# Running products of the forget gates: two scan instructions for a pair of heads in place of twelve products by doubling

## The chip, the cores and the metric

The kernel runs on one core of a Trainium2 chip. The metric is the device time of one launch in microseconds; before the change the median of three timed runs is 845.55 us (845.29 to 845.63). In the profile the engines are PE (matrix products; PEld is its weight load), DVE (vector), ACT (activation), POOL (general purpose) and SP, which here only issues transfers.

## The reference

Two layers over 512 tokens of width 1024, inner width 2048. Layer 0 is a pooling mixer. Layer 1, in which the change lies, is a gated linear recurrence (HGRN2) with 16 heads of 128 channels:

```python
def hgrn2_mixer(h, w_in, lb, norm_g, w_out):
    u = h @ w_in
    q, fz, i, gate = jnp.split(u, 4, axis=-1)
    log_f = jnp.logaddexp(jnp.log(lbf), jnp.log1p(-lbf) + jax.nn.log_sigmoid(fz))  # f = lb + (1 - lb) * sigmoid(fz)
    k = (1.0 - lbf) * jax.nn.sigmoid(-fz)
    ...
    # o_t = S_t^T q_t,  S_t = diag(f_t) S_{t-1} + k_t v_t^T, for each head, v = i
    o = hgrn2_chunk_scan(qc, kc, vc, bc)
    o = o * rsqrt(mean(o * o, over the head) + EPS) * norm_g
    return (o * jax.nn.silu(gate)) @ w_out
```

Around each mixer there are an RMSNorm before it and a residual addition after it, and a last RMSNorm.

## The kernel before

Activations lie with channels on the 128 partitions and the 512 tokens along the free axis. Each large product of float32 numbers is done as three products of exact halves (`mm3`, L126 to L128). Weights come in pieces of 128x1024 that SP loads (`wraw`), that ACT casts to the high half (`whi`, L94), and from which DVE subtracts it for the low half (`wlo`, L95). A piece's load and split carry a priority 300 traced instructions ahead of their use (`AHEAD`).

The program is written in an order, and a planner (the Tile layer) then lays down each engine's queue from the order, the dependences and the priorities; every engine works its own queue in order.

Layer 1 goes over four groups of four heads. `prepare(g)` makes what the heads of group g need: `forget` projects the gates' inputs, applies two sigmoids (ACT, L338 and L340) and lets `store` write the gates `f` (DVE, L505, L506, L508; POOL L507); then come the running products of `f`; then `queries` projects q. `group(g)` projects the values (`inputs`), runs the heads (`within` L549 to L558, `state`, `attend`), and, behind the first two heads' `gated`, calls `prepare(g + 1)`. `prepare(0)` stands alone ahead of the first group. Output products of the group before (`project_out`, the `z1` halves) fill PE meanwhile.

Tokens are taken in four blocks of 128, each with two halves of 64. Within a block the decay is a ratio to the block's middle, so the first half needs the products of the gates from t + 1 to the middle (backwards), the second those from the middle to t (forwards). Before the change these are made in place by doubling, for a pair of heads at a time: for h = 1, 2, 4, 8, 16, 32 one product for the first halves (L519) and one for the second (L520), each on 256 elements a partition, twelve in all. What follows reads them: POOL copies the products over whole halves to `ends` (L524, L525) and multiplies by the block's first gate (`e`, L527); POOL clips them at `FLOOR` (L533), DVE takes the reciprocal `r` (L534); `f` and `r` then scale k (POOL, L536 and L537) and q (DVE, L538 and L539), which the heads' first products on PE (L549) take.

Of the kernel before, what the change touches and what calls it, by code (L numbers as in the profile page):

```python
"""Two-layer streaming-encoder trunk: multi-scale causal pooling mixer, then HGRN2, on one core.

Activations are kept channel-major ([channel, token]), so every projection contracts over
partitions.  float32 products with long moving operands run as three one-pass float32r products of
exact halves (x = hi + lo, 12 significant bits each): hi*hi + hi*lo + lo*hi.  Short ones run as
plain float32 products.

The RMSNorm factor of a token commutes with the projection, so it is applied where the projection's
result leaves PSUM.

HGRN2 is computed as causal linear attention.  The decay between tokens s < t is the product of the
forget gates of s+1..t.

Factored form: within a block of 128 tokens the decay is a ratio of products taken to the block's middle,
one factor going to k and one to q; from block to block the state is carried.  The products over half a
block must not run out of range for this; whether they did is recorded on the way.

General form, for any gates, run over the layer when the record says so: a pair is served at the one
level h (1, 2, 4, ..) at which s and t lie in sibling blocks of h tokens; the decay is then (s to the end
of its block) * (start of t's block to t), both at most one, so nothing can overflow.  The running products  # L20
are lengthened from level to level by the sibling's total.
"""
# [10 lines left out]
F32 = mybir.dt.float32  # L33
# [4 lines left out]
ALU = mybir.AluOpType  # L38
PSUM = bass.MemoryType.PSUM

P = 128
# [3 lines left out]
KD = D // P          # 8 channel tiles of the model width  # L45
KI = DI // P         # 16 channel tiles of the inner width
NG = 4               # groups of the inner width
GC = DI // NG        # 512 channels a group
GT = GC // P         # 4 channel tiles a group
TB = T // P          # 4 token blocks  # L50
# [4 lines left out]
NORM_AT, SPREAD_AT = (KD - 2, 2), (KD - 1, 1)   # where in its first projection (step, tile)  # L55
AHEAD = 300           # how far, in traced instructions, the weights run ahead of their use
FLOOR = 1e-26         # the least product of gates over half a block that the factored form takes
LEVELS = (1, 2, 4, 8, 16, 32, 64)

# columns of the packed parameters  # L60
# [5 lines left out]
def trunk(ctx: ExitStack, tc: tile.TileContext, xT, par, ident_d, causal_d, mask_d, w0_in, w0_grp, w0_out, w1_in, w1_out, outT):  # L66
# [9 lines left out]
    # ---- parameters and constants  # L76
    ones = const.tile([P, P], F32, name="ones")
    nc.gpsimd.memset(ones, 1.0)
    # the tensor engine's clock comes up, and the function table in, while the first loads are on their way
# [17 lines left out]
    def piece(src):  # L97
        """A [128, 2, 512] piece of a weight as exact halves."""
        raw = wpool.tile([P, 2, GC], F32, name="wraw", tag="wraw", bufs=RAW)
        hi = wpool.tile([P, 2, GC], F32R, name="whi", tag="whi", bufs=WB)  # L100
        lo = wpool.tile([P, 2, GC], F32R, name="wlo", tag="wlo", bufs=WB)
        with tc.high_priority(AHEAD):
            nc.sync.dma_start(out=raw, in_=src)
            split(raw, hi, lo)
        return hi, lo

    def load_in(w, col=0):
        """512 columns of a projection: one pair of halves a row tile."""
        v = w.rearrange("(k p) n -> p k n", p=P)
        out = []  # L110
        for i in range(v.shape[1] // 2):
            hi, lo = piece(v[:, 2 * i:2 * i + 2, col:col + GC])
            out += [(hi[:, 0], lo[:, 0]), (hi[:, 1], lo[:, 1])]
        return out

    def load_out(w, g):
        """Rows of group g of a [2048, 1024] projection, one row tile a piece."""
# [12 lines left out]
    def project4(pieces, xs, norm):  # L130
        """The four channel tiles of 512 columns, advancing together through the contraction.  The norm's
        short products go in before the end, so that its result is there in time."""
# [11 lines left out]
    def project(pieces, n, xs):  # L144
        """[128 channels, 512 tokens] of a projection: columns n*128.. of the pieces."""
# [6 lines left out]
    def rms(name, srcs, cols=slice(0, T)):  # L152
        """1/rms of each token over the channel tiles, [token, block]."""
# [29 lines left out]
    def spread(rn):  # L183
        """[token, block] -> [any channel, token], in PSUM."""
# [31 lines left out]
    # ---- layer 0: pooling mixer  # L216
# [83 lines left out]
    # kept for the general form of the next layer  # L300
# [4 lines left out]
    # ---- layer 1: HGRN2 mixer  # L305
    # lower bounds of this layer: softmax over the layers, cumulated, less the first
# [14 lines left out]
    def hgrn(ctx, general):  # L321
# [4 lines left out]
        # attention weights within a token block: zeroed once, later only the causal part is written  # L326
# [16 lines left out]
        def forget(g, store):  # L343
            wf = None if g == 0 else load_in(w1_in, DI + g * GC)
            fs, ks = [], []
            for pr in range(2):
                f = l1.tile([P, 2, T], F32, name="f", tag="f", bufs=2)
# [46 lines left out]
        def normed(o, so):  # L394
            """Each token of a head divided by its rms; so is left with the sums of squares."""
# [13 lines left out]
        def gated(g, n, on, gate, last):  # L409
            """Back to [channel, token], times the norm's weight and the gate."""  # L410
# [14 lines left out]
        def group(g, prepare, heads, zs):  # L425
            """One group of heads: the rest of its projections, its heads, and the output products of the
            group before, which keep the tensor engine busy meanwhile."""
# [19 lines left out]
        def finish(zs):  # L447
            """Last output product and final norm, one half of the tokens after the other."""
# [11 lines left out]
            def scaled(half, i, bc, rb):  # L460
                """Two channel tiles of the result; the first two by way of the engines that are free."""
# [27 lines left out]
        def factored():  # L489
            """Decays within a block of 128 tokens as ratios to its middle; between blocks by the state.  # L490
            Returns how many of the marks that say that the ratios stayed in range are set."""
# [8 lines left out]

            def store(f, pr, j, hd, s1):
                """In a block's first half at t the gate of t + 1 (one in the middle), in the second that of t."""
                s, fv = halved(s1), halved(f[:, j])
                a = dict(scalar1=rest[:, hd:hd + 1], scalar2=low[:, hd:hd + 1], op0=ALU.mult, op1=ALU.add)
                nc.vector.tensor_scalar(out=fv[:, :, 0, 0:63], in0=s[:, :, 0, 1:64], **a)  # L505
                nc.vector.tensor_scalar(out=fv[:, :, 1, :], in0=s[:, :, 1, :], **a)  # L506
                nc.gpsimd.memset(fv[:, :, 0, 63:64], 1.0)  # L507
                nc.vector.tensor_scalar(out=cur["first"][pr][:, j], in0=s[:, :, 0, 0], **a)  # L508

            def prepare(g):  # L510
                cur["first"] = firsts = [l1.tile([P, 2, TB], F32, name="first", tag="first", bufs=2) for _ in range(2)]
                es = []
                fs, ks = forget(g, store)
                for pr in range(2):
                    f, kk = fs[pr], ks[pr]
                    for hh in (1, 2, 4, 8, 16, 32):
                        x = f.rearrange("p j (b s m two h) -> p (j b) s m two h", b=TB, s=2, two=2, h=hh)
                        n = 32 // hh
                        nc.vector.tensor_tensor(out=x[:, :, 0, :, 0], in0=x[:, :, 0, :, 0], in1=x[:, :, 0, :, 1, 0:1].broadcast_to([P, 2 * TB, n, hh]), op=ALU.mult)  # L519
                        nc.vector.tensor_tensor(out=x[:, :, 1, :, 1], in0=x[:, :, 1, :, 1], in1=x[:, :, 1, :, 0, hh - 1:hh].broadcast_to([P, 2 * TB, n, hh]), op=ALU.mult)  # L520
                    # products over the halves, the first with the block's first gate as well
                    en = ends[:, g * GT + 2 * pr:g * GT + 2 * pr + 2]
                    fv = f.rearrange("p j (b s c) -> p j b s c", b=TB, s=2)
                    nc.gpsimd.tensor_copy(out=en[:, :, :, 0], in_=fv[:, :, :, 0, 0])  # L524
                    nc.gpsimd.tensor_copy(out=en[:, :, :, 1], in_=fv[:, :, :, 1, 63])  # L525
# [4 lines left out]
                for pr in range(2):  # L530
                    for j in range(2):
                        r = l1.tile([P, T], F32, name="r", tag="r", bufs=2)
                        nc.gpsimd.tensor_scalar(out=r, in0=fs[pr][:, j], scalar1=FLOOR, scalar2=None, op0=ALU.max)  # L533
                        nc.vector.reciprocal(out=r, in_=r)  # L534
                        rv, fv, kv, qv = halved(r), halved(fs[pr][:, j]), halved(ks[pr][:, j]), halved(qs[pr][:, j])
                        nc.gpsimd.tensor_tensor(out=kv[:, :, 0], in0=kv[:, :, 0], in1=fv[:, :, 0], op=ALU.mult)  # L536
                        nc.gpsimd.tensor_tensor(out=kv[:, :, 1], in0=kv[:, :, 1], in1=rv[:, :, 1], op=ALU.mult)  # L537
                        nc.vector.tensor_tensor(out=qv[:, :, 0], in0=qv[:, :, 0], in1=rv[:, :, 0], op=ALU.mult)  # L538
                        nc.vector.tensor_tensor(out=qv[:, :, 1], in0=qv[:, :, 1], in1=fv[:, :, 1], op=ALU.mult)  # L539
                cur["k"], cur["q"], cur["e"] = ks, qs, es  # L540

            def within(n):
                """Weights within the blocks; the tokens after the middle do not weigh on those before."""
# [229 lines left out]
```

## Time and profile before

| | |
|---|---|
| median of three timed runs | 845.55 us (845.29 to 845.63) |
| the profiled execution: span from its first to its last instruction | 844.7 us |
| so between the profiled span and the median | 0.85 us |
| instructions in the profile | 10684 |
| busy share of the span | PE 98%, PEld 82%, DVE 65%, ACT 33%, POOL 20% |
| HBM traffic | 92 GB/s over the span |

The span is what the views below divide up; the timed runs contain a little more than it. Busy shares are means over the whole span. Matrix products overlap, so PE is busy also where one product follows the other at the slower of two paces.

### The profile page before, as it was taken

The numbers are of one execution on the slowest core, as the hardware profiler recorded it, in microseconds if no ns is written. First come the engines' busy times: TensorE is split into PE (matmuls) and PEld (weight loads), VectorE is DVE, ScalarE is ACT, GpSimd is POOL, SyncE is SP. The second block draws the span as 40 slices with busy tenths as digits, with TensorE's granted clock in tenths as the row PEclk, the third lists the DMA queues.
The fourth block names the chain that finished last, engine by engine and source line by source line (L and its number), as shares of the span: only waits on it lengthen the run. The fifth ranks groups of instructions, "written<-read, shape, count | busy, mean of one in ns | idle before, by whom it ended". The sixth has DMA issues, their size and how long they took to land.

```text
span 844.7 us, 10684 instructions
## 1 busy us (share of the span) xinstructions
PE 829.0 (98%) x4134; PEld 691.7 (82%) x4134; DVE 550.5 (65%) x845; ACT 274.6 (33%) x472; POOL 171.7 (20%) x218
## 2 busy tenths in 40 slices
PE   9899999999999999999999999999999999999995
PEld 7688888888888888888888888888888888888895
DVE  7766645754685465799269963279963279963643
ACT  7352224213333144323332232332332332334231
POOL 5020001001002023170314300315300305203024
PEclk9999999999999999999999999999999999999997
DMA  6622333123423145133033331233331133320203
GB/s 217 209 70 84 99 100 100 55 96 100 150 99 100 54 163 180 57 95 105 1 100 100 100 100 30 71 100 100 99 101 39 62 100 100 100 100 1 74 2 104
DMA packets 37931, 78.56 MB, mean 93 GB/s; under 512 B 2800, under 2 KB 5104, under 8 KB 37872
## 3 DMA queue, kind: packets, MB, share of 16 engines
q1 hardware_dynamic: 35744, 74.98, 27.9%
q10 hardware_dynamic: 2128, 2.81, 0.9%
q8 instruction: 34, 0.56, 0.3%
q14 instruction: 25, 0.20, 0.1%
HBM read 73.59 MB, written 4.19 MB: 92 GB/s over the span
## 4 chain that ended last, share of the span: by engine, by line
PE 91%; DVE 4%; DMA 2%; POOL 1%; issue 1%; ACT 1%; SPq 0%; ACTq 0%; DVEq 0%; POOLq 0%
PE mm L126 28%; PE mm L128 27%; PE mm L127 27%; PE a L587 2%; DVE wlo L95 1%; PE a L549 1%; PE a L589 1%; PE a L567 1%; DVE r L534 1%; DMA wraw<-in_w0i 1%; PE a L414 1%; PE a L556 1%; DMA h<-in_xT 0%; DMA wraw<-in_w1i 0%; PE a L188 0%
## 5 line engine op out<-in xcount | busy, mean ns | idle before, releaser
L126 PE MATMUL mm<-xh,whi 128*128 128x512 f32 x640 | 251.3, 393 | 0.9 <-DVE v L242 0.4
L128 PE MATMUL mm<-xh,wlo 128*128 128x512 f32 x640 | 249.8, 391 | 1.6 <-DVE wlo L95 1.6
L127 PE MATMUL mm<-xl,whi 128*128 128x512 f32 x640 | 249.6, 390 | 0.0
L94 ACT CAST whi<-wraw 128x1024 fp32r<-128x1024 f32 (+1 forms) x140 | 141.8, 1025 | 249.8 <-PE mm L127 168.9
L95 DVE TENSOR_TENSOR wlo<-wraw,whi 128x1024 fp32r<-128x1024 f32 (+1 forms) x140 | 173.4, 1265 | 58.2 <-ACT whi L94 57.2
L128 PEld LDWEIGHTS mm<-xh,wlo 128*128 128x128 f32 x640 | 120.4, 188 | 28.6 <-DVE wlo L95 3.2
L126 PEld LDWEIGHTS mm<-xh,whi 128*128 128x128 f32 x640 | 120.6, 188 | 26.6 <-ACT whi L94 1.1
L127 PEld LDWEIGHTS mm<-xl,whi 128*128 128x128 f32 x640 | 120.5, 188 | 24.5
L214 DVE TENSOR_TENSOR h<-mm,h 128x512 f32<-128x512 f32 x56 | 38.5, 689 | 62.8 <-PE mm L128 62.5
L534 DVE RECIPROCAL r<-r 128x512 f32<-128x512 f32 x16 | 53.5, 3341 | 1.5 <-POOL r L533 1.5
L126 PE MATMUL mm<-zh,whi 128*128 128x512 f32 x128 | 50.4, 394 | 0.0
L128 PE MATMUL mm<-zh,wlo 128*128 128x512 f32 x128 | 50.2, 392 | 0.0
L126 PE MATMUL mm<-whi,xh 128*128 128x512 f32 x128 | 50.1, 391 | 0.0
L127 PE MATMUL mm<-wlo,xh 128*128 128x512 f32 x128 | 49.8, 389 | 0.0
L128 PE MATMUL mm<-whi,xl 128*128 128x512 f32 x128 | 49.8, 389 | 0.0
L127 PE MATMUL mm<-zl,whi 128*128 128x512 f32 x128 | 49.7, 388 | 0.0
L390 POOL TENSOR_TENSOR gs<-fz,s 128x512 f32<-128x512 f32 x16 | 20.7, 1293 | 98.6 <-ACT s L388 98.6
L272 POOL TENSOR_TENSOR gs<-gt,sg 128x512 f32<-128x512 f32 x16 | 21.2, 1328 | 91.7 <-ACT sg L270 91.5
L126 PE MATMUL mm<-z1h,whi 128*128 128x512 f32 x96 | 38.2, 398 | 0.0
L128 PE MATMUL mm<-z1h,wlo 128*128 128x512 f32 x96 | 38.0, 395 | 0.0
L127 PE MATMUL mm<-z1l,whi 128*128 128x512 f32 x96 | 38.0, 395 | 0.0
L402 POOL TENSOR_TENSOR ro<-mo,mhalf 128x4 f32<-128x4 f32 x16 | 16.2, 1015 | 104.0 <-DVE mo L400 104.0
(141 smaller groups left out, 1202.1 us busy)
## 6 DMA issues: line engine op xcount, KB each, us to landing
wraw<-in_w1i SPq DMA_DIRECT2D x64, 512.0 KB, 4.1
wraw<-in_w0i SPq DMA_DIRECT2D x28, 512.0 KB, 4.5
wraw<-in_w0o SPq DMA_DIRECT2D x16, 512.0 KB, 4.3
wraw<-in_w1o SPq DMA_DIRECT2D x16, 512.0 KB, 4.0
wraw<-in_w0g SPq DMA_DIRECT2D x8, 512.0 KB, 3.9
h<-in_xT SPq DMA_DIRECT2D x8, 256.0 KB, 5.1
wraw<-in_w0i SPq DMA_DIRECT2D x8, 256.0 KB, 5.0
hmid<-h ACTq DMA_DIRECT2D x8, 256.0 KB, 2.3
```

The source lines that it names most:

```text
L94: nc.scalar.copy(out=hi, in_=src)
L95: nc.vector.tensor_tensor(out=lo, in0=src, in1=hi, op=ALU.subtract)
L126: nc.tensor.matmul(out, lh, rh, start=start, stop=False)
L127: nc.tensor.matmul(out, lh, rl, start=False, stop=False)
L128: nc.tensor.matmul(out, ll, rh, start=False, stop=stop)
L214: nc.vector.tensor_tensor(out=h[n], in0=acc, in1=h[n], op=ALU.add)
L272: nc.gpsimd.tensor_tensor(out=gs, in0=gt, in1=sg, op=ALU.mult)
L390: nc.gpsimd.tensor_tensor(out=gs, in0=gt, in1=sg, op=ALU.mult)
L402: nc.gpsimd.tensor_tensor(out=ro[:, :, 0], in0=mo, in1=mhalf[:, :TB], op=ALU.pow)
L414: nc.tensor.transpose(out=oT[:, b * P:(b + 1) * P], in_=on[:, b], identity=ident)
L534: nc.vector.reciprocal(out=r, in_=r)
L587: nc.tensor.matmul(o[:, b], Ads[pr][:, j, t], v[:, b, n * P:(n + 1) * P], start=True, stop=b == 0)
```

## The change

The twelve products give way to two `tensor_tensor_scan` instructions on DVE, each over 512 elements a partition: one runs through the first halves of both heads from the last token back, one through the second halves forwards. A scan keeps a running value: at each element it multiplies the value by `data0` and adds `data1`. At the places where a new half begins, `data0` is 0 and `data1` holds the value to start from: a constant tile `middle` (1 at each half's last token) for the backward one, and for the forward one a tile `begins` in which `store` writes each second half's first gate. The zeros are written by POOL, two memsets for a pair of heads in place of one for each head (L507). `f` is now stored half by half, all first halves and then all second halves, so that each scan's 512 elements lie together; the readers of `f`, `r` and the ends follow that layout, with as many elements as before. `store` has one instruction more on DVE (the gates for `begins`, four elements), and L506 writes 252 elements and not 256.

Three tiles of 512 floats are new in layer 1's pool (`middle`, two `begins`), each cleared once by POOL. The scratch area for dynamic DMA is set to 1024 where the program is made, so all tiles lie at other addresses than before. Comments and docstrings are gone.

```diff
-        def forget(g, store):
+        def forget(g, store, shape=[P, 2, T]):
...
-                f = l1.tile([P, 2, T], F32, name="f", tag="f", bufs=2)
+                f = l1.tile(shape, F32, name="f", tag="f", bufs=2)
...
+            middle = l1.tile([P, 2 * TB * 64], F32, name="middle")
+            nc.gpsimd.memset(middle, 0.0)
+            nc.gpsimd.memset(middle.rearrange("p (b c) -> p b c", c=64)[:, :, 63:64], 1.0)
+            begins = [l1.tile([P, 2, TB, 64], F32, name=f"begin{i}") for i in range(2)]
+            for b in begins:
+                nc.gpsimd.memset(b, 0.0)
...
-                s, fv = halved(s1), halved(f[:, j])
+                s, fv, bv = halved(s1), f[:, :, j], cur["begin"][pr][:, j]
                 a = dict(scalar1=rest[:, hd:hd + 1], scalar2=low[:, hd:hd + 1], op0=ALU.mult, op1=ALU.add)
-                nc.vector.tensor_scalar(out=fv[:, :, 0, 0:63], in0=s[:, :, 0, 1:64], **a)
-                nc.vector.tensor_scalar(out=fv[:, :, 1, :], in0=s[:, :, 1, :], **a)
-                nc.gpsimd.memset(fv[:, :, 0, 63:64], 1.0)
+                nc.vector.tensor_scalar(out=fv[:, 0, :, 0:63], in0=s[:, :, 0, 1:64], **a)
+                nc.vector.tensor_scalar(out=fv[:, 1, :, 1:64], in0=s[:, :, 1, 1:64], **a)
+                nc.vector.tensor_scalar(out=bv[:, :, 0], in0=s[:, :, 1, 0], **a)
                 nc.vector.tensor_scalar(out=cur["first"][pr][:, j], in0=s[:, :, 0, 0], **a)
...
-                    for hh in (1, 2, 4, 8, 16, 32):
-                        x = f.rearrange("p j (b s m two h) -> p (j b) s m two h", b=TB, s=2, two=2, h=hh)
-                        n = 32 // hh
-                        nc.vector.tensor_tensor(out=x[:, :, 0, :, 0], in0=x[:, :, 0, :, 0], in1=x[:, :, 0, :, 1, 0:1].broadcast_to([P, 2 * TB, n, hh]), op=ALU.mult)
-                        nc.vector.tensor_tensor(out=x[:, :, 1, :, 1], in0=x[:, :, 1, :, 1], in1=x[:, :, 1, :, 0, hh - 1:hh].broadcast_to([P, 2 * TB, n, hh]), op=ALU.mult)
+                    back, on = (f[:, s].rearrange("p j b c -> p (j b c)") for s in range(2))
+                    nc.gpsimd.memset(f[:, 0, :, :, 63:64], 0.0)
+                    nc.gpsimd.memset(f[:, 1, :, :, 0:1], 0.0)
+                    nc.vector.tensor_tensor_scan(out=back[:, ::-1], data0=back[:, ::-1], data1=middle[:, ::-1], initial=0.0, op0=ALU.mult, op1=ALU.add)
+                    nc.vector.tensor_tensor_scan(out=on, data0=on, data1=begins[pr].rearrange("p j b c -> p (j b c)"), initial=0.0, op0=ALU.mult, op1=ALU.add)
...
-    nc = bacc.Bacc("TRN2", target_bir_lowering=False, num_devices=1)
+    nc = bacc.Bacc("TRN2", target_bir_lowering=False, num_devices=1, dynamic_dma_scratch_size=1024)
```

## Rows read from the trace of the kernel before

**Rows 1.** The page's first part: busy time, share of the span, instructions.

```profile
PE 829.0 (98%) x4134; PEld 691.7 (82%) x4134; DVE 550.5 (65%) x845; ACT 274.6 (33%) x472; POOL 171.7 (20%) x218
```

**Rows 2.** Busy time in stretches: length, then each engine's us, granted clock, DMA.

```profile
0.00:40.00 40.00, 34.41 (x145) 27.25 (x146) 28.61 (x38) 22.04 (x34) 12.95 (x18) 0.96 0.65 212
40.00:390.00 350.00, 350.00 (x1557) 288.46 (x1555) 228.48 (x313) 113.08 (x141) 56.45 (x86) 1.00 0.31 99
390.00:400.00 10.00, 9.73 (x95) 8.18 (x94) 8.44 (x24) 2.77 (x5) 0.00 (x0) 1.00 0.62 205
400.00:830.00 430.00, 430.00 (x2314) 363.55 (x2313) 281.39 (x463) 135.04 (x288) 98.75 (x109) 1.00 0.23 74
830.00:844.70 14.70, 4.89 (x31) 4.31 (x29) 3.61 (x10) 1.62 (x4) 3.58 (x5) 0.65 0.37 125
345.00:390.00 45.00, 45.00 (x211) 37.07 (x210) 43.38 (x67) 15.62 (x20) 18.70 (x20) 1.00 0.21 60
```

**Rows 3.** Waits of PE: us in total, times, longest.

```profile
PE a L549 <- ACT kt L558: 0.3, 1, 0.3
```

**Rows 4.** The chain of waits, 336 to 412 us: start, us, what.

```profile
366.11 1.61 issue
...
393.50 0.39 ACT kt L558
```

**Rows 5.** DVE's groups by line and shape: busy us, mean ns of one.

```profile
L534 DVE RECIPROCAL r<-r 128x512 f32<-128x512 f32 x16 | 53.5, 3341 | 1.5 <-POOL r L533 1.5
...
L519 DVE TENSOR_TENSOR f<-f 128x256 f32<-128x256 f32 x48 | 19.9, 415 | 0.0
L520 DVE TENSOR_TENSOR f<-f 128x256 f32<-128x256 f32 x48 | 19.9, 415 | 0.0
...
L254 DVE TENSOR_TENSOR win<-v 128x512 f32<-128x512 f32 x16 | 11.0, 690 | 0.3
...
L508 DVE TENSOR_SCALAR first<-s,lb 128x4 f32<-128x4 f32 x16 | 4.5, 281 | 0.0
```

**Rows 6.** Timeline of DVE, 345 to 400 and 436 to 500 us.

```profile
386.39 0.95 DVE L538 TENSOR_TENSOR q<-q,r 128x256 f32<-128x256 f32 x1
...
458.44 0.42 DVE L519 TENSOR_TENSOR f<-f 128x256 f32<-128x256 f32 x1
...
462.13 0.42 DVE L520 TENSOR_TENSOR f<-f 128x256 f32<-128x256 f32 x1
...
483.03 0.41 DVE L539 TENSOR_TENSOR q<-q,f 128x256 f32<-128x256 f32 x1
...
490.46 3.95 DVE L95 TENSOR_TENSOR wlo<-wraw,whi 128x1024 fp32r<-128x1024 f32 x3 [4.31 <-ACT whi L94]
```

**Rows 7.** Timeline of POOL, 320 to 345 and 345 to 400 us.

```profile
322.00 1.85 POOL L329 MEMSET Ad<- 128x1024 f32 x2 [1.73 <-PE mm L128]
...
330.00 1.73 POOL L166 TENSOR_TENSOR sqa<-sqa,sq 128x512 f32<-128x512 f32 x1 [4.57 <-ACT sq L160]
...
356.89 4.36 POOL L524 COPY ends<-f 128x8 f32<-128x8 f32 x1 [14.96 <-DVE f L519]
```

**Rows 8.** Timeline of PE, 380 to 392 and 520 to 532 us.

```profile
379.95 0.39 PE L128 MATMUL mm<-whi,xl 128*128 128x512 f32 x1
...
388.79 0.39 PE L128 MATMUL mm<-whi,xl 128*128 128x512 f32 x1
389.11 0.32 PE L549 MATMUL a<-q,kk 128*64 128x128 f32 x1
...
519.66 0.39 PE L127 MATMUL mm<-z1l,whi 128*128 128x512 f32 x1
...
524.09 0.40 PE L128 MATMUL mm<-z1h,wlo 128*128 128x512 f32 x1
```

**Rows 9.** The page's costliest groups: output products of layer 1, x products.

```profile
L126 PE MATMUL mm<-xh,whi 128*128 128x512 f32 x640 | 251.3, 393 | 0.9 <-DVE v L242 0.4
...
L126 PE MATMUL mm<-z1h,whi 128*128 128x512 f32 x96 | 38.2, 398 | 0.0
```

More of the change, by code (lines that the diff above doesn't have):

```diff
@@ L511, in prepare @@
                 cur["first"] = firsts = [l1.tile([P, 2, TB], F32, name="first", tag="first", bufs=2) for _ in range(2)]
+                cur["begin"] = begins
                 es = []
-                fs, ks = forget(g, store)
+                fs, ks = forget(g, store, [P, 2, 2, TB, 64])
                 for pr in range(2):
-                    f, kk = fs[pr], ks[pr]
-                    for hh in (1, 2, 4, 8, 16, 32):
-                        x = f.rearrange("p j (b s m two h) -> p (j b) s m two h", b=TB, s=2, two=2, h=hh)
-                        n = 32 // hh
-                        nc.vector.tensor_tensor(out=x[:, :, 0, :, 0], in0=x[:, :, 0, :, 0], in1=x[:, :, 0, :, 1, 0:1].broadcast_to([P, 2 * TB, n, hh]), op=ALU.mult)
-                        nc.vector.tensor_tensor(out=x[:, :, 1, :, 1], in0=x[:, :, 1, :, 1], in1=x[:, :, 1, :, 0, hh - 1:hh].broadcast_to([P, 2 * TB, n, hh]), op=ALU.mult)
+                    f = fs[pr]
+                    back, on = (f[:, s].rearrange("p j b c -> p (j b c)") for s in range(2))
[3 more added lines that the diff above has]
+                    nc.vector.tensor_tensor_scan(out=on, data0=on, data1=begins[pr].rearrange("p j b c -> p (j b c)"), initial=0.0, op0=ALU.mult, op1=ALU.add)
                     en = ends[:, g * GT + 2 * pr:g * GT + 2 * pr + 2]
-                    fv = f.rearrange("p j (b s c) -> p j b s c", b=TB, s=2)
-                    nc.gpsimd.tensor_copy(out=en[:, :, :, 0], in_=fv[:, :, :, 0, 0])
-                    nc.gpsimd.tensor_copy(out=en[:, :, :, 1], in_=fv[:, :, :, 1, 63])
+                    nc.gpsimd.tensor_copy(out=en[:, :, :, 0], in_=f[:, 0, :, :, 0])
+                    nc.gpsimd.tensor_copy(out=en[:, :, :, 1], in_=f[:, 1, :, :, 63])
                     e = l1.tile([P, 2, TB], F32, name="e", tag="e", bufs=2)
@@ L531, in prepare @@
                     for j in range(2):
-                        r = l1.tile([P, T], F32, name="r", tag="r", bufs=2)
-                        nc.gpsimd.tensor_scalar(out=r, in0=fs[pr][:, j], scalar1=FLOOR, scalar2=None, op0=ALU.max)
+                        r = l1.tile([P, 2, TB, 64], F32, name="r", tag="r", bufs=2)
+                        f = fs[pr][:, :, j]
+                        nc.gpsimd.tensor_scalar(out=r, in0=f, scalar1=FLOOR, scalar2=None, op0=ALU.max)
                         nc.vector.reciprocal(out=r, in_=r)
[L535 to L539, printed above, removed]
+                        kv, qv = halved(ks[pr][:, j]), halved(qs[pr][:, j])
+                        nc.gpsimd.tensor_tensor(out=kv[:, :, 0], in0=kv[:, :, 0], in1=f[:, 0], op=ALU.mult)
+                        nc.gpsimd.tensor_tensor(out=kv[:, :, 1], in0=kv[:, :, 1], in1=r[:, 1], op=ALU.mult)
+                        nc.vector.tensor_tensor(out=qv[:, :, 0], in0=qv[:, :, 0], in1=r[:, 0], op=ALU.mult)
+                        nc.vector.tensor_tensor(out=qv[:, :, 1], in0=qv[:, :, 1], in1=f[:, 1], op=ALU.mult)
                 cur["k"], cur["q"], cur["e"] = ks, qs, es
```

## The prediction

> **What bounds the kernel now.** I first read the page's busy times: PE works 829.0 of 844.7 us, DVE 550.5 [rows 1]. Both look busy, so the question is where PE stands still, and who makes it. The table by stretches answers that: PE is idle 40.00 - 34.41 = 5.59 us in the first 40 us, 10.00 - 9.73 = 0.27 us from 390 to 400, and 14.70 - 4.89 = 9.81 us behind 830 us; in the 350 us and the 430 us between there is no idle time at all [rows 2]. The three gaps make 15.67 us, the whole of 844.7 - 829.0. The head is layer 0's first loads and the tail the last norm and stores; neither has a forget gate in it. Layer 1 with its four calls of `prepare` lies between, so what the change can take from PE's idle time is the 0.27 us from 390 to 400.
>
> PE's own waits name that gap: the heads' first product of a group waits once, for 0.3 us, for ACT's copy `kt` [rows 3]. The chain of waits shows how the delay came about. It leaves PE at 366.11 us and runs over DVE (the reciprocals and q's products among it), then over a weight piece's load and cast, to that copy at 393.50 us [rows 4]. From 345 to 390 us DVE is busy 43.38 of 45.00 us, with PE at 45.00 of 45.00 in the same stretch [rows 2]. So in group 0, where `prepare(0)` has no heads of an earlier group beside it, DVE has just enough time; it holds PE up by 0.3 us and no more. That is the only place where faster products help, and a place where slower ones would hurt.
>
> **Removed.** 96 products (48 of L519, 48 of L520) of 415 ns: 39.8 us of DVE's busy time [rows 5]. Their ends overlap the next one's start; in the queue twelve take 12/11 of (462.13 - 458.44) = 4.03 us a pair of heads [rows 6].
>
> **Added: scans.** Sixteen over 512 elements. No row shows a scan. From below its cost is bounded by the nearest form, a product of two operands over 512 elements: 690 ns [rows 5]. From above I take DVE's slowest instruction over 512 elements, the reciprocal: 3341 ns [rows 5]. Between them: 415 ns for 256 and 690 for 512 give 275 ns for each 256 elements and 140 ns fixed. In a scan an element needs the value of the one before it, which a product doesn't, so I double the part that grows: 140 + 4 x 275 = 1240 ns, an estimate from those two rows and nearer to the product than to the reciprocal. It makes 16 x 1.24 = 19.8 us (11.0 to 53.5 at the bounds). [...]
>
> **Added: small ones.** Sixteen more gate instructions of four elements, at L508's 281 ns: 4.5 us [rows 5]. DVE's sum is -39.8 + 19.8 + 4.5 = -15.5 us, to about 535.0 us of busy time (526.2 to 568.7 at the bounds).
>
> POOL writes the zeros with as many memsets as before (two for a pair of heads), now ahead of a scan, so DVE waits for them; queued behind the scan on DVE are the next heads' gates and weight halves. The memsets need only a free `f` and POOL idles 14.96 us before it copies the first ends [rows 7], so they cost nothing; without that cover a memset would stand behind POOL's other work and hold DVE up, by the longest of these rows 4.36 us [rows 7], about what groups 1 to 3 can bear (below). Clearing the three new tiles is 3 x 512 elements at the 1.85 us that 2 x 1024 took: 1.4 us, in a stretch where POOL idles 4.57 us before its next sum of squares [rows 7]: nothing; uncovered it would delay the norm by 1.4 us. The readers of `f` in its new layout have as many instructions and elements as before: nothing added; if the layout made them slower, the slack worked out next would pay for it. No transfer is added or moved.
>
> **What that is worth on the path.** A pair of heads costs DVE's queue 2 x 1.24 + 2 x 0.28 = 3.04 us in place of 4.03, so a group 2.0 us less. In group 0 the last product of q ends at 386.39 + 0.95 = 387.34 us and the heads' first product starts at 389.11 [rows 6, 8]: already 1.77 us of slack, and PE has products to do until then. What was late was the weight half behind q in DVE's queue, and with it the load, the cast and `kt`; 2.0 us earlier they are in time, and the 0.3 us go. Nothing is late next, since PE has no other gap before 830 us. In group 1 q is ready at 483.03 + 0.41 = 483.44 us, and DVE then idles 4.31 us up to 490.46, waiting for ACT [rows 6]; there, and in groups 2 and 3 which repeat it, 2.0 us less DVE only lengthen that idle time. On the path: -0.3 us. The profiled span would go from 844.7 to 844.4, and with the 0.85 us between the span and the median the time from 845.55 to 845.2 us. Below 0.2%, 1.7 us, a measurement of this kernel can hardly tell a difference from none; this is one fifth of that.
>
> **The rivals.**
>
> *The scans are so slow that group 0 stalls (slower).* Group 0's queue time changes by 2 x (2s + 0.56 - 4.03) us for a scan of s us. It eats up the 1.77 us of slack at 4s = 1.77 + 6.94, s = 2.18 us; from there PE waits. At the reciprocal's 3.34 us it is 6.4 - 1.8 = 4.6 us more in group 0, and 850.2 us in all; groups 1 to 3 take 6.4 us more out of the 4.31 us of idle time and the weights' lead without holding PE up. For it: the recurrence, and a DVE that is full in that stretch. Against it: s would have to be over three times the product's 0.69. 0.05.
>
> *The tiles' new places change PE's own pace (faster, or slower).* PE isn't at one pace. The values' products of group 0 follow each other at (388.79 - 379.95)/39 = 0.2267 us (39 steps), the output products at (524.09 - 519.66)/19 = 0.2332 us (19 steps) [rows 8]; means of 393 and 398 ns say the same of all of them [rows 9]. Nothing in the rows says why, and the change moves every tile. If the 3 x 96 products with `z1` [rows 9] came to the faster pace, 288 x 0.0065 = 1.9 us would go besides the 0.3: 843.3 us. If the 3 x 640 products with x took the slower one, 12.5 us would come: 858 us. For it: a difference that holds for a whole stage. Against it: no row ties it to a place in memory. 0.13 for the gain, 0.03 for the loss.
>
> *DVE's saving comes through whole (faster).* 845.55 - 15.5 = 830 us. For it: DVE at 65%, full for tens of us in each group. Against it: PE has no idle time in the 780 us that it would have to come out of [rows 2]. 0.02.
>
> *A new order in the queues.* The planner sees 24 - 4 - 4 = 16 fewer DVE instructions a group, and weights run 300 traced instructions ahead of use, so splits of weights slip earlier in DVE's queue by about that. A split too early stands in front of q and waits for its transfer. The 1.77 us of group 0 and the 4.31 of the others bound what is free; I expect less than 1 us either way, inside "no change", with 0.02 for more in each direction.
>
> *The change doesn't do what it says:* were the scans' products out of range, the general form would run as well (the `If` at L725), a second pass through layer 1 and far outside any range here. The products are the same ones. 0.01.
>
> **How the numbers follow.** No measurable change, as worked out: 0.72. Faster by over 0.2%: 0.13 + 0.02 + 0.02 = 0.17. Slower: 0.05 + 0.03 + 0.02 + 0.01 = 0.11. The likeliest gives 845.2 us, with its own range from 844.3 to 846.2 for the queues' new order. The 8-in-10 range goes down to 843.0, so that the `z1` products' pace is in it, and up to 847.2, where a stall of group 0 begins to show; the reciprocal's price and the slower x products stay outside.
>
> **What would show it.** Right: scans of 1.1 to 1.4 us; DVE's busy time near 535 us, PE's still near 829; no wait of L549 for `kt` and no idle PE from 390 to 400 us; the chain of waits on PE all through layer 1; DVE's idle time before the weight halves behind q longer by about 2 us a group. Wrong: scans over 2.2 us with a wait of PE on q or k in group 0 (the first rival); a pace of `z1` products of 0.227 or of x products above 0.230 us (the second); a PE wait at L549 in groups 1 to 3, or DVE waiting for POOL's memsets ahead of a scan for more than a few tenths of a us. The time would also come out wrong if the tail behind 830 us changed, which nothing in the change touches.

## The result and the profile after

The changed kernel takes 850.72 us (median of four runs, 849.66 to 852.9) against 845.59 us for the kernel before beside it (845.29 to 847.14). The ratio is 1.0059 with an interval from 1.0045 to 1.0073: slower by about 0.6%, where 845.2 us was predicted. The profiled execution took 849.71 us with a span of 847.8 us.

Most single steps came out as worked out. The page's busy times of the kernel after:

```profile
PE 829.6 (98%) x4134; PEld 690.8 (81%) x4134; DVE 534.7 (63%) x781; ACT 275.8 (33%) x472; POOL 165.6 (20%) x222
```

DVE has 15.8 us less to do than before [rows 1], against 15.5 predicted, and PE's work has not grown. DVE's groups of the new lines (busy us, mean ns of one):

```profile
L530 DVE TENSOR_TENSOR_SCAN f<-f,begin 128x512 f32<-128x512 f32 x8 | 10.0, 1244 | 0.0
L529 DVE TENSOR_TENSOR_SCAN f<-f,middle 128x512 f32<-128x512 f32 x8 | 9.7, 1216 | 0.0
L515 DVE TENSOR_SCALAR begin<-s,lb 128x4 f32<-128x4 f32 x16 | 5.3, 329 | 0.0
```

A scan costs 1.22 to 1.24 us; the estimate was 1.24. What remains above the 140 ns taken as fixed is 1.08 to 1.10 us, twice the product's 0.55.

So the loss is not in the new instructions' own time. The stretches of the kernel after show where PE stands still (columns as in [rows 2]):

```profile
0.00:40.00 40.00, 34.39 (x150) 27.95 (x151) 29.62 (x40) 21.95 (x34) 11.82 (x18) 0.96 0.63 219
...
390.00:400.00 10.00, 10.00 (x90) 8.55 (x87) 8.36 (x26) 2.50 (x5) 0.00 (x0) 1.00 0.43 147
400.00:830.00 430.00, 427.75 (x2286) 359.35 (x2286) 262.46 (x405) 135.83 (x287) 93.23 (x106) 1.00 0.23 73
```

The 0.27 us between 390 and 400 us went, as predicted. But between 400 and 830 us, where PE had worked without a pause [rows 2], 2.25 us of idle time are new. Cut into stretches of 10 us, they sit in three places, one for each of groups 1 to 3:

```profile
470.00:480.00 10.00, 9.25 (x41) 7.02 (x40) 10.00 (x11) 1.06 (x1) 1.92 (x2) 1.00 0.44 148
600.00:610.00 10.00, 9.25 (x40) 7.03 (x39) 9.97 (x15) 2.54 (x4) 1.58 (x1) 1.00 0.62 190
720.00:730.00 10.00, 9.24 (x45) 7.39 (x45) 9.70 (x6) 3.17 (x3) 4.92 (x4) 1.00 0.01 2
```

PE's waits name the line; the wait for `kt` [rows 3] is gone and this one has come (us in total, times, longest):

```profile
PE mm L127 <- DVE wlo L95: 2.2, 3, 0.8
```

PE's timeline of group 1 shows the wait inside the values' projection, at its fifth product with a low half, that is, at the third of the value weights' four pieces:

```profile
469.92 0.48 PE L126 MATMUL mm<-whi,xh 128*128 128x512 f32 x1
...
472.73 0.39 PE L126 MATMUL mm<-whi,xh 128*128 128x512 f32 x1
473.87 0.50 PE L127 MATMUL mm<-wlo,xh 128*128 128x512 f32 x1 [0.75 <-DVE wlo L95]
...
475.13 0.40 PE L126 MATMUL mm<-whi,xh 128*128 128x512 f32 x1
475.53 0.50 PE L127 MATMUL mm<-wlo,xh 128*128 128x512 f32 x1
```

From product to product it should be 0.23 us, as from 474.37 to 474.60 us in the kernel before. Here it is 473.87 - 472.73 = 1.14, and at the next piece 475.53 - 475.13 = 0.40: 1.1 us lost, more than the 0.75 us that the views call idle, because a product counts as busy while it ends: its row lasts 0.39 us, though the next one can start 0.23 us behind it.

What DVE did just then, in the kernel after:

```profile
445.07 3.35 DVE L544 RECIPROCAL r<-r 128x512 f32<-128x512 f32 x1 [3.17 <-POOL r L543]
...
466.17 6.56 DVE L544 RECIPROCAL r<-r 128x512 f32<-128x512 f32 x2 [0.30 <-POOL r L543]
472.65 3.96 DVE L95 TENSOR_TENSOR wlo<-wraw,whi 128x1024 fp32r<-128x1024 f32 x3
```

And in the kernel before, in lines of the view of [rows 6] that the prediction did not draw on:

```profile
469.40 3.34 DVE L534 RECIPROCAL r<-r 128x512 f32<-128x512 f32 x1
472.66 3.97 DVE L95 TENSOR_TENSOR wlo<-wraw,whi 128x1024 fp32r<-128x1024 f32 x3
...
477.82 3.34 DVE L534 RECIPROCAL r<-r 128x512 f32<-128x512 f32 x1
```

This is the difference. Before, DVE's queue held the third reciprocal, then three low halves of weights, then the fourth reciprocal. After, the third and the fourth stand together, and the three halves come behind both. The first two of the three belong to the third and the fourth value piece. The two executions do not reach this stage at the same time of their spans, so the halves are timed against the first product of the values, which starts at 471.31 us before and at 469.92 after. In the kernel before, the fifth product with a low half starts at 474.37 us:

```profile
471.31 0.48 PE L126 MATMUL mm<-whi,xh 128*128 128x512 f32 x1
...
474.37 0.39 PE L127 MATMUL mm<-wlo,xh 128*128 128x512 f32 x1
```

The halves begin 472.66 - 471.31 = 1.35 us behind the first product before, and 472.65 - 469.92 = 2.73 us after. They come 1.4 us later, though DVE has less to do. Before, the first of them was done at about 473.9 us, so about 0.5 us was to spare.

A second thing changed: DVE now waits for POOL's clip, 10.4 us in all where it was 1.5 [rows 5], and 3.17 + 0.30 us of it in this stretch of group 1:

```profile
L544 DVE RECIPROCAL r<-r 128x512 f32<-128x512 f32 x16 | 53.1, 3336 | 10.4 <-POOL r L543 10.4
```

The chain of waits of the kernel after leaves PE at exactly this place; before it ran on PE alone from 425 to 500 us (start, us, what):

```profile
467.97 1.47 issue
469.44 3.29 DVE r L544
472.73 1.09 DVE wlo L95
473.82 0.04 issue
473.87 0.50 PE mm L127
```

Two theories were left to tell apart: the order of DVE's queue, or something that the scans brought with them (their tiles, the layout of `f`, the smaller scratch area).

### The profile page after: what moved, and what is told of

It is laid out like the page before. It is cut to its first block, busy times and chain, and to the rows that moved or that the text cites. A ratio compares the mean times of both kernels' runs of the same rounds, so it can differ in the third digit from the quotient of the medians.

```text
span 847.8 us, 10626 instructions
## 1 busy us (share of the span) xinstructions
PE 829.6 (98%) x4134; PEld 690.8 (81%) x4134; DVE 534.7 (63%) x781; ACT 275.8 (33%) x472; POOL 165.6 (20%) x222
## 4 chain that ended last, share of the span: by engine, by line
PE 92%; DVE 3%; issue 1%; POOL 1%; DMA 1%; ACT 1%; ACTq 0%; DVEq 0%; POOLq 0%
PE mm L127 28%; PE mm L126 28%; PE mm L128 28%; PE a L559 2%; PE a L597 2%; PE a L599 1%; PE a L577 1%; DVE r L544 1%; DVE wlo L95 1%; PE a L566 1%; PE a L414 1%; POOL sqa L166 0%; PE a L188 0%; DMA wraw<-in_w0i 0%; DMA pp<-in_par 0%
## 5 line engine op out<-in xcount | busy, mean ns | idle before, releaser
L95 DVE TENSOR_TENSOR wlo<-wraw,whi 128x1024 fp32r<-128x1024 f32 (+1 forms) x140 | 170.0, 1240 | 66.2 <-ACT whi L94 65.2
L544 DVE RECIPROCAL r<-r 128x512 f32<-128x512 f32 x16 | 53.1, 3336 | 10.4 <-POOL r L543 10.4
```

The costliest lines, as they stand in the source:

```text
L95: nc.vector.tensor_tensor(out=lo, in0=src, in1=hi, op=ALU.subtract)
```

## The experiments

The measure that the experiments share is the time from the first to the last product of the values in each of groups 1 to 3, read from PE's timeline of the profiled executions:

| kernel | group 1 | group 2 | group 3 | median, us | before beside it |
|---|---|---|---|---|---|
| before | 21.67 | 21.63 | 21.66 | 845.59 | |
| after | 22.95 | 22.96 | 23.04 | 850.72 | 845.59 |
| after, once more | 23.02 | 23.01 | 23.02 | 850.41 | 845.56 |
| after, reciprocal put back | 21.63 | 21.63 | 21.63 | 846.03 | 845.56 |
| before, halves put behind | 26.66 | 26.40 | 25.32 | 859.95 | 845.56 |
| before, smaller scratch area | 21.66 | 21.63 | 21.66 | 845.67 | 845.56 |
| before, six products | 25.71 | 25.67 | 25.62 | 856.04 | 845.84 |
| after, put back in group 1 alone | 21.63 | 23.02 | 22.97 | 848.59 | 845.84 |
| after, put back, scans twice | 23.82 | 23.83 | 23.82 | 864.03 | 845.84 |

### The reciprocal put back behind the halves

```diff
-                        nc.vector.reciprocal(out=r, in_=r)
+                        if g and pr and j:
+                            early.append(load_in(w1_in, 2 * DI + g * GC))
+                            with tc.issue_after(lows[-1].ins):
+                                nc.vector.reciprocal(out=r, in_=r)
+                        else:
+                            nc.vector.reciprocal(out=r, in_=r)
```

`lows` collects the instructions of L95, and `inputs` takes the pieces loaded here, so the value pieces' loads and splits are also written ahead of the fourth reciprocal. Everything else of the change stays.

> The changed kernel with one thing put back: in groups 1 to 3 the group's fourth reciprocal is queued on DVE behind the low halves of the value weights, as it stood in the kernel before; the scans stay. Theory (the new order of DVE's queue): in the changed kernel PE stands 1.2 to 1.4 us at the values' products in each of the three groups, for the low halves come after two reciprocals in a row; with the order back these waits are gone, PE has no idle time from 400 to 830 us, and the time falls by 3 x 1.3 = 3.9 us from 849.7 to about 846, as fast as the kernel before within 0.2%. Rival (the tiles' new places and the smaller scratch area): the time stays at 849.7 to 851. Second rival (the scans hold POOL or DVE up): the time stays as well, with waits of PE at the same products.

Measured: 846.03 us (844.18 to 848.61, 11 runs), ratio to before 1.0002 (0.9992 to 1.0011). The kernel after, run on the same chip, gave 850.41 us (848.93 to 851.9), ratio 1.0050 (1.0036 to 1.0064); its expectation was

> The changed kernel once more beside the others. All theories: 849.7 to 853 us, with PE waits of 0.75 us and more at the values' products of groups 1 to 3.

With the order put back, 850.41 - 846.03 = 4.4 us return. Two of DVE's halves now stand ahead of the fourth reciprocal:

```profile
470.93 2.35 DVE L95 TENSOR_TENSOR wlo<-wraw,whi 128x1024 fp32r<-128x1024 f32 x2
473.20 3.34 DVE L551 RECIPROCAL r<-r 128x512 f32<-128x512 f32 x1
```

and PE has no pause left in the 430 us:

```profile
400.00:830.00 430.00, 430.00 (x2320) 364.04 (x2319) 265.71 (x411) 137.08 (x290) 95.89 (x110) 1.00 0.24 75
```

DVE is busy 535.3 us here, 15 us less than before, and the time is that of before: on PE's path the saving is worth nothing. DVE's waits for POOL's clip are as long here as in the kernel after (10.4 us in all, 3.18 and 0.30 in this stretch), so these waits alone do not make the loss.

### The kernel before with the halves behind the reciprocal

```diff
+            n = len(lows)
             wi = load_in(w1_in, 2 * DI + g * GC)
+            if g and not general:
+                for low_half in lows[n + 2:]:
+                    tc.add_manual_dep(low_half.ins, last_r[0].ins.name, ...)
...
-                        nc.vector.reciprocal(out=r, in_=r)
+                        last_r[:] = [nc.vector.reciprocal(out=r, in_=r)]
```

No scan, no new tile, the same places in memory; the edit only queues the low halves of the last two value pieces behind the fourth reciprocal.

> The kernel before, with its twelve products by doubling and its tiles where they were, and only the order of DVE's queue changed: in groups 1 to 3 the fourth reciprocal is queued ahead of the low halves of the last two pieces of the value weights. Theory (order): PE waits for them in three groups, by 2 to 4.5 us each as DVE is 2 us a group later here than with the scans: 852 to 859 us. Rivals (places, scans): neither is in this kernel, so 845.6 us as before.

Measured: 859.95 us (857.74 to 861.48), ratio 1.0168 (1.0148 to 1.0189), a little above the range. PE's wait is the one of the kernel after, three times:

```profile
PE mm L129 <- DVE wlo L95: 9.3, 3, 3.1
```

The order makes the wait without any scan, and with 1.4 us of waits for POOL's clip, about as many as before. By the table it costs 4.5 us a group (the mean of 26.66, 26.40 and 25.32, less 21.65) and not only the 3.1 of the wait. In groups 1 and 2 PE is also slower for a while behind the wait; PE's timeline and the stretches of group 1 show it:

```profile
477.12 0.50 PE L129 MATMUL mm<-wlo,xh 128*128 128x512 f32 x1 [3.09 <-DVE wlo L95]
...
478.58 0.63 PE L128 MATMUL mm<-whi,xh 128*128 128x512 f32 x1
479.01 0.63 PE L129 MATMUL mm<-wlo,xh 128*128 128x512 f32 x1
```

```profile
475.00:480.00 5.00, 2.88 (x9) 2.21 (x10) 5.00 (x5) 0.00 (x0) 1.59 (x1) 0.81 0.30 105
480.00:485.00 5.00, 5.00 (x20) 4.01 (x19) 4.43 (x8) 2.67 (x4) 0.00 (x0) 0.85 0.64 210
```

About 1 us behind the wait the products follow each other at 0.43 us and not 0.23, from 478.15 to 481.56 us, and then at 0.23 to 0.24 again. The granted clock (last column but two) is 0.81 and 0.85 in these two stretches, and 1.00 in the 5 us before them and in the 5 us behind them. In group 2 the products from 608.91 to 611.04 us, just behind the wait, are 0.43 us apart. In group 3 the wait is as long, but the products behind it are not 0.43 us apart (0.23 from 741.49 to 741.72 us); this group loses 25.32 - 21.66 = 3.7 us where the other two lose 5.0 and 4.8:

```profile
739.25 0.50 PE L129 MATMUL mm<-wlo,xh 128*128 128x512 f32 x1 [3.08 <-DVE wlo L95]
...
741.49 0.39 PE L128 MATMUL mm<-whi,xh 128*128 128x512 f32 x1
741.72 0.40 PE L129 MATMUL mm<-wlo,xh 128*128 128x512 f32 x1
```

So the length of the wait does not settle by itself whether the products slow down behind it. In the kernel after, with waits of 0.75 us, the granted clock is 1.00 in the three stretches of 10 us around them.

### The smaller scratch area alone

```diff
-    nc = bacc.Bacc("TRN2", target_bir_lowering=False, num_devices=1)
+    nc = bacc.Bacc("TRN2", target_bir_lowering=False, num_devices=1, dynamic_dma_scratch_size=1024)
```

This moves the tiles of the kernel before and does nothing else.

> The kernel before with the scratch area set to 1024 and nothing else, so that every tile lies 15 KB lower and the queues are as before. Theory (order): the time stays at 845.6 us within 0.2%, with PE's paces as they were. Rival (places and scratch): it rises by the 1 us by which the span and the time have drawn apart, or by more, to 846.6 to 850 us.

Measured: 845.67 us (845.19 to 847.12, 12 runs), ratio 0.9999 (0.9990 to 1.0007). The move of all tiles costs and brings nothing. The first experiment, which shows no loss, has the new tiles and the smaller scratch area of the kernel after as well.

### Half of the products, by doubling

```diff
-                    for hh in (1, 2, 4, 8, 16, 32):
+                    for hh in (1, 2, 4):
```

> The kernel before (doubling, old layout, no scan, no new tile) with the loop over h cut from 1, 2, 4, 8, 16, 32 to 1, 2, 4: it leaves out half of the running products, so the decays it computes are those over eight tokens at most; DVE does 6 products a pair of heads, about 2.0 us, a group 4.0 us less than before. Its DVE queue, as built, has the fourth reciprocal ahead of the three low halves of the value weights in groups 1 to 3, as the changed kernel has. Queue theory (whatever shortens the running products lets the reciprocal slip ahead of the halves, scan or not): the halves come 3.3 us later for the reciprocal and 2.0 us earlier for the six products of the pair ahead of it, or up to 4.0 us earlier if both pairs count, so between 0.7 us earlier and 1.3 us later than before; with 0.6 us to spare PE waits 0 to 0.8 us in each group, and the time is 845.5 to 849, above before if the wait appears. Rival (the loss belongs to the scans, the new layout or the new tiles): none of them is in this kernel, DVE has 20 us less to do, so 845.2 to 845.6 with no wait at the values' products.

Measured: 856.04 us (854.29 to 857.98), ratio 1.0110 (1.0095 to 1.0126). With about 21 us taken from DVE (529.5 us busy) and no scan, the kernel is slower by 10.2 us. So the rival falls: to shorten the products is enough here, without a scan, the new layout or a new tile. The size was missed, though: the measured time lies 7 us above the range. DVE's and PE's timelines say why:

```profile
467.68 3.35 DVE L534 RECIPROCAL r<-r 128x512 f32<-128x512 f32 x1 [1.38 <-POOL r L533]
470.95 0.63 DVE L366 TENSOR_TENSOR q<-mm,rb 128x512 f32<-128x512 f32 x1
471.49 3.34 DVE L534 RECIPROCAL r<-r 128x512 f32<-128x512 f32 x1
474.75 3.96 DVE L95 TENSOR_TENSOR wlo<-wraw,whi 128x1024 fp32r<-128x1024 f32 x3
```

```profile
475.96 0.50 PE L127 MATMUL mm<-wlo,xh 128*128 128x512 f32 x1 [2.13 <-DVE wlo L95]
...
477.79 0.63 PE L127 MATMUL mm<-wlo,xh 128*128 128x512 f32 x1
478.22 0.63 PE L128 MATMUL mm<-whi,xl 128*128 128x512 f32 x1
```

The third reciprocal waits 1.38 us for POOL's clip, and in the whole kernel such waits make 15.9 us, where they made 1.5 before [rows 5]. What the products no longer take turns into waiting there, while the halves still stand behind a further reciprocal: they begin 474.75 - 470.63 = 4.1 us behind the first product of the values, against 1.35 before. And behind the wait the products slow down, here in all three groups: they are 0.43 us apart from 477.36 to 480.35 us, from 607.00 to 609.99 and from 737.14 to 739.70. The granted clock is 0.71 from 475 to 480 us and 0.95 from 480 to 485.

### The order put back in one group

```diff
-                        if g and pr and j:
+                        if g == 1 and pr and j:
```

> The changed kernel with the fourth reciprocal put behind the low halves in group 1 alone; groups 2 and 3 keep the planner's order. Queue theory, each group paying for its own order: one third of what the order costs comes back, (850.41 - 846.03)/3 = 1.5 us, so 848.9 (848.3 to 849.5), with two waits at the values' products of low halves left, of 0.75 us each. Rival (the delay is handed on from group to group, or one early group decides): either all of it comes back, 846, or none, 850.4.

Measured: 848.59 us (847.43 to 850.77, 10 runs), ratio 1.0034 (1.0024 to 1.0044). Group 1 has its 21.63 us again, groups 2 and 3 keep 23.0 us, and PE's waits show two where there were three:

```profile
PE mm L129 <- DVE wlo L95: 1.5, 2, 0.7
```

Each group pays for its own order. The rival of this run, that the delay is handed on, falls.

### Each scan twice, with the order put back

```diff
+                    nc.vector.tensor_tensor_scan(out=spare[:, ::-1], data0=back[:, ::-1], data1=middle[:, ::-1], ...)
                     nc.vector.tensor_tensor_scan(out=back[:, ::-1], data0=back[:, ::-1], data1=middle[:, ::-1], ...)
+                    nc.vector.tensor_tensor_scan(out=spare, data0=on, data1=begins[pr]..., ...)
                     nc.vector.tensor_tensor_scan(out=on, data0=on, data1=begins[pr]..., ...)
```

> The changed kernel with the fourth reciprocal behind the low halves, as in the first experiment, and each scan issued a second time, before the real one, into a tile that nothing reads: 16 scans and 19.7 us more on DVE, 555 us in all. If DVE is the bound on the way to the low halves, as its 32.70 of 32.70 busy us from 440 us to the halves say, a pair of heads costs 4 x 1.23 + 0.56 = 5.5 us in place of 4.03 before, a group 2.9 us more, of which 0.6 us are spare and up to 3 us may be idle time behind the first reciprocal: PE waits 0 to 2.3 us in groups 1 to 3, and 2.9 - 1.8 = 1.1 us in group 0 at the heads' first product: 847 to 854. If the idle time of 4.3 us behind q was the slack of groups 1 to 3, as the prediction had it, they take the 2.9 us without a wait and only group 0 pays: 846.5 to 847.

Measured: 864.03 us (863.5 to 864.82), ratio 1.0212 (1.0198 to 1.0226): above both expectations. PE's waits are for low halves again, at more places (three of the six at L130, 1.6 us, lie in layer 0):

```profile
PE mm L129 <- DVE wlo L95: 9.4, 5, 2.7
PE mm L130 <- DVE wlo L95: 4.8, 6, 1.1
```

In group 0 PE waits twice, and the granted clock from 370 to 380 us is 0.87; in group 1 it waits once in the projection of q (L130) and once in that of the values:

```profile
371.73 0.50 PE L129 MATMUL mm<-wlo,xh 128*128 128x512 f32 x1 [1.02 <-DVE wlo L95]
376.07 0.50 PE L129 MATMUL mm<-wlo,xh 128*128 128x512 f32 x1 [2.68 <-DVE wlo L95]
...
459.08 0.50 PE L130 MATMUL mm<-xh,wlo 128*128 128x512 f32 x1 [1.06 <-DVE wlo L95]
...
483.99 0.50 PE L129 MATMUL mm<-wlo,xh 128*128 128x512 f32 x1 [1.89 <-DVE wlo L95]
```

```profile
370.00:380.00 10.00, 6.29 (x22) 4.42 (x21) 10.00 (x9) 1.73 (x2) 3.14 (x3) 0.87 0.42 114
```

DVE is busy 558.7 us, so 23.4 us more on DVE cost 864.03 - 846.03 = 18 us, though 15 us less bring nothing. The groups do not have 4.3 us to spare. The planner also placed other halves and reciprocals of this kernel differently than in the first experiment, so the 18 us are not the price of DVE's time alone; how they divide stays open.

## Why the prediction was wrong

**Right.** The scans' price, DVE's sum (534.7 us, 535.0 predicted), PE's unchanged work, the memsets and clears at no cost, and group 0: the wait for `kt` and PE's idle time from 390 to 400 us went. That the growing part of a scan is twice a product's was the author's assumption, which no row of the kernel before shows; the scans of the kernel after took 1216 and 1244 ns, where it gave 1240. The paces of PE did not change (393 ns for the products with x, 398 for `z1`, as in [rows 9]), so that rival falls, together with the one of slow scans. Right too is that a DVE saving cannot show where PE has no pause: with the order put back the kernel is at the time of before. And DVE's idle time before the halves behind q did grow, from 4.31 us to 7.32 in group 1; but PE needed the slack elsewhere:

```profile
490.31 1.22 DVE L95 TENSOR_TENSOR wlo<-wraw,whi 128x1024 fp32r<-128x1024 f32 x1 [7.32 <-ACT whi L94]
```

One term of the sum compares unlike things and does no harm. The 0.85 us between the span and the median takes the span from one execution and the median from others; in the runs that have both, an execution's time is 1.75 to 2.04 us above its own span. The 845.2 us are 845.55 less 0.3 and do not need it.

**The step that failed** is the sentence on groups 1 to 3: "there, and in groups 2 and 3 which repeat it, 2.0 us less DVE only lengthen that idle time". It has two faults. First, the 4.31 us of idle time that end at 490.46 us [rows 6] lie over 10 us behind the deadline that counts: the third value piece's low half, due at the values' fifth product with a low half, at 474.37 us. Up to the halves DVE had been busy in all of 440 to 472.66 us, and the half was there about 0.5 us before PE asked for it. Slack must be read at the instruction for which PE will ask next, not at the next gap in an engine's timeline. Second, it took DVE's queue as given and moved it forward as a whole. The planner lays the queue down anew for each kernel, and here an instruction of 3.34 us [rows 5] went past three of about 1.3 us, two of which PE needed at once.

**The rival that came true** was there: "A new order in the queues". Its price was mis-sized: "I expect less than 1 us either way", from the 4.31 us. Measured, the values' projection takes 1.33 us longer in each group (the mean of 22.95, 22.96 and 23.04, less 21.65), 4.0 us in three groups. The kernel after lost 850.72 - 845.59 = 5.1 us in one comparison and 850.41 - 845.56 = 4.9 in the other, and the order put back returned 4.4. The intervals of the two ratios go from 3.8 to 6.2 and from 3.0 to 5.4 us, so the 4.0 lie inside both; whether something further is lost besides is not shown. The direction was mistaken as well: the argument was about weight halves that slip *earlier* and stand in front of q; what happened is that they slipped *behind* a reciprocal. The first rival's 850.2 us lie near the measured time by chance: its cause, slow scans that stall group 0, did not come.

**By the signs that the prediction set:** the chain of waits was to stay on PE through layer 1, and it leaves it at 467.97 us for a reciprocal and a low half. DVE waits in the kernel after also for POOL's clip, 3.17 us at 445.07, with weight halves queued behind the waiting reciprocal; no such wait was among the signs, which looked only for the memsets. The first experiment has the same waits and no loss, and the second has the loss with hardly any of them, so the order is what decides between the kernels at hand. What the kernel after would take with its order and without these 3.5 us a group, more than the 1.4 by which the halves are late, no run shows.

**Why the planner chose so** was only argued: it plans with its own costs, and with shorter products a reciprocal's input is ready sooner in its plan, so it takes the reciprocal first. The half-doubling kernel has the same order and no scan, which fits; the planner's reasons no run shows.

## What to carry to other kernels

Before a saving on an engine with spare time is called harmless, look for what else stands in that engine's queue with a deadline, and read the slack at the instruction that is asked for next. Where a planner lays down the queue, a shorter instruction is also a new order; compare the two queues around the long instructions (here a reciprocal of 3.3 us) before comparing times, and pin the order where a short instruction feeds the bound engine. An engine at 65% can be without slack in one stretch of each group and idle in the rest.

## What the runs showed of the hardware

A scan of 512 float32 elements a partition takes 1216 to 1244 ns on average in the kernel after, where a product of two operands takes 690 [rows 5]. In the values' projections of the experiments PE waited seven times for 2.1 to 3.1 us. Behind five of these waits (three with six products, two with the halves put behind), at once or about 1 us later, products followed each other at 0.43 us and not 0.23, for 2.1 to 3.4 us. In group 1 the granted clock was 0.71 and 0.95 in the 5 us up to 480 us and the 5 us behind with six products, and 0.81 and 0.85 with the halves put behind. With the scans twice it was 0.87 in the 10 us around the wait of 2.68 us and 0.96 in the next 10. Behind the seventh, of 3.08 us, products were 0.23 us apart, and around waits of 0.75 us in the kernel after, and of 1.06 and 1.89 us in group 1 with the scans twice, the granted clock was 1.00. So a wait of PE cost up to 5.0 us where its row in the list of waits says 3.1.
